# The last product of a two-block layer by Strassen's scheme, with a wider 31-tap convolution and the third mixer moved ahead

## The chip, the cores and the metric

One core of one Trainium2 chip runs the kernel. The metric is the device time of one launch in microseconds (us). A median of three launches is given for the kernel before.

## The reference

Two blocks follow one another on x (1024 tokens by 1024 channels, fp32). The first is a hybrid attention layer with an MLP. The second, which the change touches, reads

```python
proj = h @ w_in_2                                  # 1024 x 1024 times 1024 x 5632, eleven slots of 512
(va, za, bb, bc, bv, zb, ca, cg, zc, dv, zd) = split(proj, 11)
ya = rglru(va);  yb = bb * conv3(bc * bv)
yc = silu(layer_norm(conv31(ca * sigmoid(cg)))) @ c_pw + c_pw_b
yd = (grouped product of pool_grid(dv)) * d_scale
cat = concat([ya * silu(za), yb * silu(zb), yc * silu(zc), yd * silu(zd)])   # 1024 x 2048
x = x + gate * (cat @ w_out_2)                     # 1024 x 2048 times 2048 x 1024: the last product
return rms_norm(x, final_g)
```

The four mixers are called a, b, c and d; c, the third, holds the 31-tap convolution, the layer norm and the product with `c_pw`.

## The kernel before, in words

Channels lie on the 128 partitions and tokens on the free axis, in two halves of 512. Every fp32 product is taken as three float32r matmuls: an operand is split into a high part (a copy on ACT that rounds) and a low part (a subtraction on DVE), and high times high, high times low and low times high go into one PSUM bank (`mm3_steps`, lines 411 to 413). So each 128x128 block of weights costs three matmuls per half of the tokens, and each 128x1024 tile of weights costs one split (`split`, L367 on ACT and L368 on DVE) after a 512 KB load on SP's queue (`load_raw`, L372). `take` keeps one tile of weights prepared ahead in the order of `weight_order`; three raw and three split tiles exist.

`mixers_in` makes the eleven slots: 44 column blocks, each a projection `p2` of 8 x 3 matmuls per half. The work of the mixers is laid between them by hand: generators stand in two lists, and after each projection `fill(FA, FB)` lets the first list, `self.bg` (mixers a and d, chunk by chunk), run for FA units and the second, `convs` (four 31-tap convolutions), for FB. A generator yields the units that a step stands for. `conv31` (L1986 to L1997) holds its two accumulators of 128x512 in PSUM (`pp`, five banks), makes two instructions of DVE a tap (L1994), 30 taps after the first, and copies the result back over its input on ACT. Mixer c starts when the loop over mixer b reaches its last chunk: what is left of the convolutions is run out, then `mixer_c` goes on `self.bg`, and what is not done by the end goes on in the last product. The framework orders the instructions of each engine by this program order and by when they are ready; instructions marked `pin` keep their place.

All mixers store 128x512 tiles of `cat` in DRAM (`cat_out`, `cat_store`; a factor 0.5 belongs to the silu). `tail` is the last product: `dense(pair, hf, ticks)` loads eight `cat` tiles (L2196, `cr`), splits them (`cx`, L467 and L468), and for each of eight column blocks n makes one projection of 24 matmuls and adds it, times the gate (`MOD`), to x (L2208). Two pairs of mixers, (a, d) and (b, c), and two halves of the tokens give four calls, 32 projections, 768 matmuls. x comes back from DRAM by `load_x` (`x2d`); the second pair also sums squares (`add_sq`, L1362 and L1363); `final` normalises (L2218) and stores. The product of the MLP earlier in the kernel already goes by Strassen's scheme, with sums of weight blocks made by `weight_sums`: a DMA on GpSimd's queue (POOL) loads a block into the one tile `ws`, others add to it in flight, and others store the sums to DRAM (L1490, L1494, L1496). `pace` emits one of these DMAs per projected half. 32 tiles of 128x1024 (`S`) and small pools of eight (`T2`) and six (`F2`) 128x512 tiles hold everything.

Of the kernel before, what the change touches and what calls it, by code (L numbers as in the profile page):

```python
# [17 lines left out]
P = 128  # L18
# [10 lines left out]
NL, N1, N2, N4, N3, FA, FB = 6.0, 3.0, 3.0, 2.4, 2.5, 4.0, 3.0  # L29
# [272 lines left out]
class Build:  # L302
    def __init__(self, tc, ctx, A, out, dbg=None):
# [16 lines left out]
        self.sums, self.paced = self.weight_sums(), 0  # L320
# [54 lines left out]
    def load_w(self, src, w=T):  # L375
# [3 lines left out]
        self.split(raw[:, :w], hi[:, :w], lo[:, :w])  # L379
        return hi, lo  # L380

    def weight_order(self):
# [9 lines left out]
        q += [("wo2", pair, n) for pair in range(2) for hf in range(2) for n in range(8)]  # L392
        self.wq, self.ahead = q, []

    def take(self, *key):
        if self.wq[0] is None:
            self.wq.pop(0)
        assert self.wq.pop(0) == key
        load = lambda name, *i: self.load_w(self.A[name][i] if name == "wup" else
                                               self.A[name][i].rearrange("p k n -> p (k n)"))  # L400
# [1079 lines left out]
    def weight_sums(self):  # L1480

        nc = self.nc
        A = self.A["wm2"]
        self.ws = {n: [self.dp.tile([P, T], F32, name=f"{n}w{j}") for j in range(8)] for n in ("S1", "S2", "S3", "S4")}
        pin = self.tc.keep_in_program_order
        for j in range(8):
            block = lambda a, b: A[a, b][:, j * T:j * T + T]
            for first, *terms in (((1, 0), (1, 1), "S1", (0, 0), "S2", (0, 1), "S4"), ((0, 0), (1, 0), "S3")):
                t = self.wsp.tile([P, T], F32, tag="ws", name=self.nm("ws"))
                pin(nc.gpsimd.dma_start(t, block(*first)))  # L1490
                yield
                for x in terms:
                    if isinstance(x, str):
                        pin(nc.gpsimd.dma_start(self.ws[x][j], t))  # L1494
                    else:
                        pin(nc.gpsimd.dma_start(t, block(*x), accum_op=ALU.add))  # L1496
                    yield
# [470 lines left out]
    def cat_out(self, i, c, y, z, hf):  # L1968
# [3 lines left out]
        self.nc.vector.scalar_tensor_tensor(t, y, 0.5, t, op0=ALU.mult, op1=ALU.mult)  # L1972
        self.cat_store(i, c, t, hf)

# [5 lines left out]
    def conv31(self, c, u):  # L1980

        nc = self.nc
        w = lambda j: self.CW[:, 31 * c + j:31 * c + j + 1]
# [250 lines left out]
def run(gen):  # L2234
    for _ in gen:
        pass
# [48 lines left out]
```

## Time and profile before

| | us |
|---|---|
| median of 3 launches (lowest, highest) | 2552.47 (2544.95, 2559.07) |
| the profiled launch | 2546.38 |
| its span, first to last instruction | 2544.6 |
| PE busy | 2462.2 (97%) |
| DVE busy | 1726.1 (68%) |
| ACT busy | 1193.8 (47%) |
| POOL busy | 181.9 (7%) |

PE is TensorE, PEld its weight loads, DVE is VectorE, ACT is ScalarE, POOL is GpSimd, SP is the engine that issues most DMAs. A matmul's row is longer than the time until the next one starts, since they are pipelined, so a pace is read from starts and not from durations. The mean granted clock of TensorE is 0.984 of full speed, 1.00 in all windows from 1813 us until the last matmul.

### The profile page before, as it was taken

To read this page: it belongs to the slowest core of one execution; us is meant where nothing else is said; L and a number is where in the kernel's file an instruction comes from. 1 tells how busy PE (TensorE), PEld (TensorE's weight loads), DVE (VectorE), ACT (ScalarE), POOL (GpSimd) and SP (SyncE) were. 2 spreads that over 40 slices of the span, in tenths; PEclk is the share of its full clock that TensorE was granted. 3 is DMA by queue.
4 is the path that set the end of the run, shared out by engine and by line. 5 is a ranking of instruction groups with operands and counts; after the bars stand their busy time and mean duration, and the time that the engine had idled before them with its cause. 6 is when DMAs were issued, how large, how long until landed. Compare 5 with 4: busy or idle time off the path is not lost. (4 is left out here: it accounts for less than half of the span.)

```text
span 2544.6 us, 33697 instructions
## 1 busy us (share of the span) xinstructions
PE 2462.2 (97%) x12692; PEld 1996.6 (78%) x12692; DVE 1726.1 (68%) x2647; ACT 1193.8 (47%) x1848; POOL 181.9 (7%) x238
## 2 busy tenths in 40 slices
PE   8989999999989999999999999999999999999997
PEld 6878898777777678877788888887888888887786
DVE  7537566574755436758867864468798999996744
ACT  6425554622514358146744543435536355445623
POOL 0000000120211111630000000000000000000000
PEclk9989999999999999999999999999999999999999
DMA  6364453584774567859676565556533333325732
GB/s 223 105 212 138 129 152 114 163 242 118 218 220 145 184 208 235 301 174 281 229 263 223 173 212 169 195 184 229 186 117 113 133 134 98 112 92 195 243 100 100
DMA packets 180084, 449.23 MB, mean 177 GB/s; under 512 B 32144, under 2 KB 42256, under 8 KB 179920
## 3 DMA queue, kind: packets, MB, share of 16 engines
q1 hardware_dynamic: 141504, 342.44, 40.7%
q0 software_dynamic: 18576, 64.63, 9.2%
q10 hardware_dynamic: 19840, 40.00, 4.2%
q8 instruction: 100, 1.64, 0.3%
q14 instruction: 64, 0.52, 0.1%
HBM read 321.55 MB, written 125.44 MB: 176 GB/s over the span
## 5 line engine op out<-in xcount | busy, mean ns | idle before, releaser
L367 ACT CAST wh<-wr 128x1024 fp32r<-128x1024 f32 (+1 forms) x243 | 254.8, 1049 | 481.6 <-PE mm L412 231.1
L368 DVE TENSOR_TENSOR wl<-wr,wh 128x1024 fp32r<-128x1024 f32 (+1 forms) x243 | 298.6, 1229 | 180.9 <-ACT wh L367 172.4
L411 PE MATMUL mm<-h,wh 128*128 128x512 f32 x736 | 301.2, 410 | 7.1 <-ACT h L467 4.3
L412 PE MATMUL mm<-h,wh 128*128 128x512 f32 x736 | 298.0, 405 | 0.0
L413 PE MATMUL mm<-h,wl 128*128 128x512 f32 x736 | 295.9, 402 | 0.3 <-DVE wl L368 0.3
L411 PE MATMUL mm<-kk,wh 128*128 128x512 f32 x704 | 275.2, 391 | 0.0
L412 PE MATMUL mm<-kk,wh 128*128 128x512 f32 x704 | 274.5, 390 | 0.5 <-DVE kk L1784 0.5
L413 PE MATMUL mm<-kk,wl 128*128 128x512 f32 x704 | 274.0, 389 | 0.0
L411 PEld LDWEIGHTS mm<-h,wh 128*128 128x128 f32 x736 | 141.8, 193 | 39.7 <-ACT h L467 5.9
L412 PEld LDWEIGHTS mm<-h,wh 128*128 128x128 f32 x736 | 141.8, 193 | 32.4 <-issue 3.6
L1994 DVE SCALAR_TENSOR_TENSOR pp<-cu,vec,pp 128x512 f32<-128x512 f32 (+9 forms) x240 | 166.7, 749 | 0.1
L413 PEld LDWEIGHTS mm<-h,wl 128*128 128x128 f32 x736 | 141.1, 192 | 32.6 <-issue 1.8
L412 PEld LDWEIGHTS mm<-kk,wh 128*128 128x128 f32 x704 | 132.1, 188 | 29.2 <-issue 1.0
L411 PEld LDWEIGHTS mm<-kk,wh 128*128 128x128 f32 x704 | 132.1, 188 | 28.3 <-issue 0.7
L413 PEld LDWEIGHTS mm<-kk,wl 128*128 128x128 f32 x704 | 132.1, 188 | 27.6 <-issue 0.2
L1512 PE MATMUL pp<-h,wh 128*128 128x512 f32 x320 | 127.1, 400 | 3.0 <-ACT x L1579 2.2
L1513 PE MATMUL pp<-h,wh 128*128 128x512 f32 x320 | 125.0, 391 | 1.4 <-DVE h L468 1.4
L1514 PE MATMUL pp<-h,wl 128*128 128x512 f32 x320 | 123.9, 390 | 0.0
L1721 PE MATMUL pp<-bl,wh 128*128 128x512 f32 x304 | 119.3, 392 | 2.3 <-DVE bl L468 1.6
L1722 PE MATMUL pp<-bh,wl 128*128 128x512 f32 x304 | 118.4, 389 | 0.0
L1720 PE MATMUL pp<-bh,wh 128*128 128x512 f32 x304 | 116.4, 391 | 1.6 <-ACT bh L472 1.6
L411 PE MATMUL mm<-cx,wh 128*128 128x512 f32 x256 | 99.8, 391 | 1.3 <-ACT cx L467 1.3
(559 smaller groups left out, 5453.2 us busy)
## 6 DMA issues: line engine op xcount, KB each, us to landing
wr<-in_wi_dram SPq DMA_DIRECT2D x77, 512.0 KB, 3.7
ws<-in_wm_dram POOLq DMA_DIRECT2D x48, 512.0 KB, 5.9
wr<-in_wo_dram SPq DMA_DIRECT2D x48, 512.0 KB, 3.7
wr<-in_wg_dram SPq DMA_DIRECT2D x32, 512.0 KB, 4.6
gt<-gt POOLq DMA_DIRECT2D x64, 256.0 KB, 3.6
g<-gt SPq DMA_DIRECT2D x64, 256.0 KB, 5.2
wm<-in_wm_dram SPq DMA_DIRECT2D x32, 512.0 KB, 5.0
br<-buB SPq DMA_DIRECT2D x32, 512.0 KB, 4.5
```

Of the source, the lines that this page charges most:

```text
L367: self.nc.scalar.copy(hi, raw)
L368: self.nc.vector.tensor_sub(lo, raw, hi.bitcast(F32))
L411: M(ps, lhsT=ah, rhs=bh, start=start and i == 0, stop=False)
L412: M(ps, lhsT=ah, rhs=bl, start=False, stop=False)
L413: M(ps, lhsT=al, rhs=bh, start=False, stop=stop and i == last)
L1512: M(ps, lhsT=ah, rhs=bh, start=start and i == 0, stop=False, skip_group_check=True)
L1513: M(ps, lhsT=ah, rhs=bl, start=False, stop=False, skip_group_check=True)
L1514: M(ps, lhsT=al, rhs=bh, start=False, stop=i == last, skip_group_check=True)
L1720: M(banks[p], lhsT=wh[:, o], rhs=bh[:, r], start=first, stop=False, skip_group_check=True)
L1721: M(banks[p], lhsT=wh[:, o], rhs=bl[:, r], start=False, stop=False, skip_group_check=True)
L1722: M(banks[p], lhsT=wl[:, o], rhs=bh[:, r], start=False, stop=jj == 7 and e == 1, skip_group_check=True)
L1994: nc.vector.scalar_tensor_tensor(o, u[:, a + s:b + s], w(j), o, op0=ALU.mult, op1=ALU.add)
```

## The change

Four edits.

1. **The last product.** `cat` and `w_out` are cut into 2 x 2 blocks: rows by pair of mixers, columns of tokens by half, columns of the output by half. Seven products P1, P5, P2, P6, P7, P4, P3 of 4 column blocks x 8 x 3 matmuls take the place of eight. The sums of weight blocks (S1 to S4) are made by `weight_sums`, now with its count and block as arguments, in DRAM during `mixers_in`. The sums of `cat` blocks are made by DMAs: SP loads a tile, and a DMA on POOL's queue adds the other block to it. Four of the sixteen block quarters are stored with the other sign (`half_of`). Products are added to x straight from PSUM, each wherever it belongs (`add`): P1 to three places, P5 to two, the others to one. P2 is accumulated in the banks of P1, and P7 and P4 in those of P6.
2. **The convolution.** One accumulator of 128x1024 in SBUF (`co`), one instruction of up to 1024 columns a tap; the first tap is ACT's; the copy back goes.
3. **The third mixer.** `mixer_c` stands in `convs` behind the four convolutions; what is left at the end goes to `self.bg`.
4. **The rates.** FA 4.0 to 4.2, FB 3.0 to 4.4.

```diff
-NL, N1, N2, N4, N3, FA, FB = 6.0, 3.0, 3.0, 2.4, 2.5, 4.0, 3.0
+NL, N1, N2, N4, N3, FA, FB = 6.0, 3.0, 3.0, 2.4, 2.5, 4.2, 4.4
...
+        src = {"P1": lambda: block(0, j), "P2": lambda: block(1, j), "P4": lambda: block(1, 4 + j),
+               "P5": lambda: self.ws["S1"][j], "P6": lambda: self.ws["S2"][j], "P7": lambda: self.ws["S3"][j],
+               "P3": lambda: self.ws["S4"][j]}[p]()
+        return self.load_w(src, minus=p == "P2")
...
-        q += [("wo2", pair, n) for pair in range(2) for hf in range(2) for n in range(8)]
+        q += [("o2", p, j) for p in ("P1", "P5", "P2", "P6", "P7", "P4", "P3") for j in range(4)]
...
-    def conv31(self, c, u):
+    def conv31(self, c, us):
...
-        acc = [self.pp(), self.pp()]
-        for hf, sl in enumerate(HS):
-            nc.vector.tensor_scalar(acc[hf], u[:, sl], w(15), None, op0=ALU.mult)
+        o = self.S("co")
+        nc.scalar.mul(o, u, w(15))
...
-            for hf in range(2):
-                a, b = max(HALF * hf, -s), min(HALF * hf + HALF, T - s)
-                o = acc[hf][:, a - HALF * hf:b - HALF * hf]
-                nc.vector.scalar_tensor_tensor(o, u[:, a + s:b + s], w(j), o, op0=ALU.mult, op1=ALU.add)
-            yield 1.3
-        for hf, sl in enumerate(HS):
-            nc.scalar.copy(u[:, sl], acc[hf])
+            a, b = max(0, -s), min(T, T - s)
+            nc.vector.scalar_tensor_tensor(o[:, a:b], u[:, a + s:b + s], w(j), o[:, a:b], op0=ALU.mult, op1=ALU.add)
+            yield 1.2
+        us[c] = o
...
+        self.sums = self.weight_sums(4, lambda a, b, j: self.A["wo2"][b, 4 * a + j].rearrange("p k n -> p (k n)"))
...
+            convs.append(self.conv31(c, cus))
+            if c == 3:
+                convs.append(self.mixer_c(cus))
...
-            if c == 3:
-                while convs:
-                    self.tick(1, convs)
-                self.behind(self.mixer_c(cus))
...
+        self.bg += convs
...
+        def source(p, k):
+            if p in ("P1", "P2", "P3", "P7"):
+                t = self.F2("cr")
+                nc.sync.dma_start(t, cat(*{"P1": (0, 0), "P2": (1, 0), "P3": (1, 1), "P7": (0, 1)}[p], k))
+                if p == "P7":
+                    nc.gpsimd.dma_start(t, cat(1, 1, k), accum_op=ALU.add)
+                return t
+            t = part(k)
+            if p == "P5" and k not in made:
+                nc.sync.dma_start(t, cat(0, 1, k))
+            elif p == "P5":
+                return t
+            made.add(k)
+            nc.gpsimd.dma_start(t, cat(*{"P5": (0, 0), "P6": (1, 1), "P4": (1, 0)}[p], k), accum_op=ALU.add)
+            return t
...
+        for k in range(8):
+            source("P5", k)
+        run(ops["P1"])
+        run(ops["P5"])
+        A = bank_a()
+        for hf in (1, 0):
+            self.load_x(x, hf, lambda hf, j: self.x2d[hf][j])
+        for j, ps in product("P1", bs["P1"], A, True, (), 5):
+            add(1, 0, j, ps)
+            add(1, 1, j, ps)
+            add(0, 1, j, ps, True)
+        for j, ps in product("P5", bs["P5"], None, True, (), 5):
+            add(1, 1, j, ps)
+            add(0, 1, j, ps, True)
         self.flush()
-        dense(1, 0, 0)
+        run(ops["P2"])
+        for j, ps in product("P2", bs["P2"], A, False, ops["P6"]):
+            add(0, 0, j, ps, True, True)
+        A = bank_a()
+        for j, ps in product("P6", bs["P6"], A, True, ops["P7"]):
+            add(0, 1, j, ps)
+        for j, ps in product("P7", bs["P7"], A, False, ops["P4"]):
+            add(1, 1, j, ps, True, True)
+        for j, ps in product("P4", bs["P4"], A, False, ops["P3"]):
+            add(1, 0, j, ps, True, True)
         self.behind(final(0))
-        dense(1, 1, 2)
+        for j, ps in product("P3", bs["P3"], None, True, (), 3):
+            add(0, 1, j, ps, True, True)
         self.flush()
         run(final(1))
```

## Rows read from the trace of the kernel before

**Rows 1.** Page, part 1: busy time, share of the span, instructions of each engine.

```profile
PE 2462.2 (97%) x12692; PEld 1996.6 (78%) x12692; DVE 1726.1 (68%) x2647; ACT 1193.8 (47%) x1848; POOL 181.9 (7%) x238
```

**Rows 2.** Windows: stretch, length, busy us and instructions by engine, clock, DMA share, GB/s.

```profile
1813.00:2334.00 521.00, 517.32 (x2263) 423.38 (x2263) 474.64 (x611) 249.49 (x330) 14.84 (x20) 1.00 0.36 121
1956.00:2276.00 320.00, 318.32 (x1399) 261.66 (x1398) 305.38 (x383) 148.84 (x197) 13.68 (x18) 1.00 0.34 116
2276.00:2334.00 58.00, 56.66 (x246) 45.65 (x245) 43.55 (x62) 28.24 (x42) 0.00 (x0) 1.00 0.35 120
2334.00:2424.00 90.00, 88.56 (x384) 71.66 (x385) 64.18 (x91) 51.09 (x76) 0.00 (x0) 1.00 0.73 255
2424.00:2529.00 105.00, 105.00 (x464) 86.56 (x462) 48.14 (x57) 30.50 (x36) 0.00 (x0) 1.00 0.28 93
```

**Rows 3.** Tile `cx`: count, duration ns min/median/max, first and last start, forms.

```profile
L411 PE MATMUL mm<-cx,wh x256: 389/389/798, 2333.9 to 2528.5; 128*128 128x512 f32 x128
L413 PE MATMUL mm<-cx,wl x256: 387/389/796, 2334.9 to 2529.0; 128*128 128x512 f32 x128
```

**Rows 4.** Timeline of PE, 30 matmuls apart: start us, duration us.

```profile
2503.16 0.39 PE L413 MATMUL mm<-cx,wl 128*128 128x512 f32 x1
...
2509.96 0.39 PE L413 MATMUL mm<-cx,wl 128*128 128x512 f32 x1
```

**Rows 5.** Chain of work that ended last, from the last epilogue.

```profile
2529.42 0.76 DVE x L2208
...
2536.92 3.98 DVE x L2218 x6
```

**Rows 6.** Groups by form, 1700 us on: busy us, mean ns, idle before.

```profile
L368 DVE TENSOR_TENSOR wl<-wr,wh 128x1024 fp32r<-128x1024 f32 x101 | 123.6, 1223 | 28.8 <-ACT wh L367 24.2 <-DMA wr<-S1w 2.9
L468 DVE TENSOR_TENSOR cx<-cr,cx 128x512 fp32r<-128x512 f32 x32 | 20.2, 687 | 5.3 <-ACT cx L467 5.3
L2208 DVE SCALAR_TENSOR_TENSOR x<-mm,MOD,x 128x512 f32<-128x512 f32 x32 | 24.0, 750 | 59.3 <-PE mm L413 59.3
```

**Rows 7.** The same view: the convolution's instructions, and a sum without PSUM.

```profile
L1994 DVE SCALAR_TENSOR_TENSOR pp<-cu,vec,pp 128x512 f32<-128x512 f32 x120 | 89.7, 753 | 0.0
L1986 DVE TENSOR_SCALAR pp<-cu,vec 128x512 f32<-128x512 f32 x8 | 5.7, 749 | 0.0
L2218 DVE SCALAR_TENSOR_TENSOR x<-x,vec,rs 128x512 f32<-128x512 f32 x16 | 11.0, 748 | 7.2 <-ACT rs L448 7.2
```

**Rows 8.** Timeline of DVE: six narrow taps in a row, and what follows.

```profile
2285.49 4.00 DVE L1994 SCALAR_TENSOR_TENSOR pp<-cu,vec,pp 128x512 f32<-128x512 f32 x6
2289.39 1.23 DVE L368 TENSOR_TENSOR wl<-wr,wh 128x1024 fp32r<-128x1024 f32 x1
```

**Rows 9.** Timeline of DVE: wide taps, first with another between, then dependent neighbours.

```profile
2205.26 1.28 DVE L1823 SCALAR_TENSOR_TENSOR xc<-va,vec,xc 128x1023 f32<-128x1023 f32 x1
2206.45 0.74 DVE L1994 SCALAR_TENSOR_TENSOR pp<-cu,vec,pp 128x502 f32<-128x502 f32 x1
...
2306.31 1.28 DVE L2052 SCALAR_TENSOR_TENSOR by<-bm,vec,by 128x1023 f32<-128x1023 f32 x1
2307.63 1.28 DVE L2053 SCALAR_TENSOR_TENSOR by<-bm,vec,by 128x1023 f32<-128x1023 f32 x1
```

**Rows 10.** Windows inside the last product, columns as in rows 2.

```profile
2340.00:2350.00 10.00, 10.00 (x46) 8.29 (x45) 5.86 (x8) 3.46 (x5) 0.00 (x0) 1.00 1.01 375
...
2390.00:2400.00 10.00, 10.00 (x46) 8.29 (x45) 5.44 (x8) 3.83 (x6) 0.00 (x0) 1.00 1.00 355
```

**Rows 11.** Lines 1496 (adding DMA) and 1490 (plain): issue ns, then landing us.

```profile
L1496 POOL DMA_DIRECT2D ws<-in_wm_dram x32: 878/922/957, 470.8 to 1188.2; - x32
...
DMA to landing us min/median/max: 5.5/6.6/9.7
...
L1490 POOL DMA_DIRECT2D ws<-in_wm_dram x16: 527/538/541, 465.3 to 1183.7; - x16
...
DMA to landing us min/median/max: 4.1/4.7/7.9
```

More of the change, by code (lines that the diff above doesn't have):

```diff
@@ L319, in __init__ @@
         self.wsp = e(tc.tile_pool(name="wsp", bufs=1))
-        self.sums, self.paced = self.weight_sums(), 0
+        self.sums, self.paced = self.weight_sums(8, lambda a, b, j: A["wm2"][a, b][:, j * T:j * T + T]), 0
     def dma(self, dst, src, q="sync"):
@@ L378, in load_w @@
         lo = self.wp.tile([P, T], F32R, tag="wl", name=self.nm("wl"))
-        self.split(raw[:, :w], hi[:, :w], lo[:, :w])
+        (self.hilo_minus if minus else self.split)(raw[:, :w], hi[:, :w], lo[:, :w])
         return hi, lo
@@ L2188, in tail @@
         accs = [None, None]
[L2190 to L2211 removed]
+        run(self.sums)
@@ new lines, in tail, with part @@
+        ng = self.sm(8)
+        nc.vector.tensor_scalar(ng, self.MOD[:, 16:24, 0], -1.0, None, op0=ALU.mult)
+        cat = lambda b, c, k: self.cat[((0, 3), (1, 2))[b][k // 4], k % 4, c]
+        ct, made = [], set()
+        def part(k):
+            if k % 2 == 0 and len(ct) <= k // 2:
+                ct.append(self.S("ct"))
+            return ct[k // 2][:, HS[k % 2]]
+        def source(p, k):
[13 more added lines that the diff above has]
+            return t
@@ new lines, in operand, with add @@
+        def operand(p, bs):
+            for k in range(8):
+                t = self.S("cx", F32R)
+                (self.hilo_minus if p in ("P7", "P4") else self.hilo)(source(p, k), t[:, 0:HALF], t[:, HALF:T])
+                bs.append(t)
+                if k % 2:
+                    yield
+        def add(a, c, j, ps, minus=False, done=False):
+            n = 4 * a + j
+            xa = x.get(n, c)
+            nc.vector.scalar_tensor_tensor(xa, ps, ng[:, n:n + 1] if minus else self.MOD[:, 16 + n, 0:1], xa,
+                                           op0=ALU.mult, op1=ALU.add)
+            if done:
+                first = accs[c] is None
+                if first:
+                    accs[c] = self.T2("acc")
+                self.add_sq(accs[c], xa, first)
@@ new lines, in product @@
+        def product(p, bs, banks, start, ahead=(), ticks=0):
+            M = nc.tensor.matmul
+            for j in range(4):
+                w = self.cols(self.take("o2", p, j))
+                ps = banks[j] if banks else self.mm()
+                for k in range(8):
+                    h, l = bs[k][:, 0:HALF], bs[k][:, HALF:T]
+                    M(ps, lhsT=w[0][k], rhs=h, start=start and k == 0, stop=False, skip_group_check=True)
+                    M(ps, lhsT=w[0][k], rhs=l, start=False, stop=False, skip_group_check=True)
+                    M(ps, lhsT=w[1][k], rhs=h, start=False, stop=k == 7, skip_group_check=True)
+                yield j, ps
+                next(iter(ahead), None)
```

62 lines of the change are left out of this document (24 added, 38 removed).

## The prediction

> **What bounds the kernel now.** The page's busy times come first [rows 1]: PE is busy 97% of the span, DVE 68%, POOL 7%. So time is to be had only from fewer matmuls or from the 3% in which PE waits. The windows then show the two stages that the change touches [rows 2]. In the mixers' stage (1813 to 2334 us) PE is busy 517.3 of 521.0 us, and in its middle DVE is nearly as full: 305.4 of 320. In the last product PE idles 1.4 of the first 90 us and nothing of the next 105, with DVE at 64.2 and 48.1. So PE bounds both stages, with DVE close behind in the first and far behind in the second. The granted clock is 1.00 in all of them, so the change can win or lose nothing there as long as PE stays busy. The chain that ended last closes with a piece that the change leaves alone: from the last epilogue at 2529.4 us to the end at 2544.6 us, 15.2 us of sums of squares, normalisation and stores [rows 5].
>
> **The matmuls.** Before, the last product has 32 projections of 24 matmuls, 768 (three lines of 256 each, first start 2333.9 us, last 2529.0) [rows 3]. After, it has 7 products x 4 x 24 = 672, so 96 go. The price of one is its pace: 30 matmuls take 2509.96 - 2503.16 = 6.80 us, 0.2267 us each [rows 4]. That is **-21.8 us**, all on the path, because PE bounds this stage. The third mixer's own matmuls move from this stage to the one before and cost the same there.
>
> **Waits that may go.** PE idles 3.7 us in the mixers' stage and 1.4 us in the last product [rows 2]. At most 5.1 us can come back. I take -2: the third mixer's chain no longer runs through the last product, and P1 needs only mixers a and d, finished earlier. **-2 us.**
>
> **Vector work of the last product, beside PE.** Sums into x go from 32 to 40 (12 for P1, 8 for P5, 4 for each other product), +8 x 0.75 = 6.0 us; operand splits from 32 to 56, +24 x 0.69 = 16.5; weight splits from 32 to 28, -4 x 1.22 = -4.9 [rows 6]. The third mixer takes away what else lies in the first 90 us: 64.2 less 16 weight splits (19.6), 32 operand splits (22.0) and 16 sums (12.0) leaves 10.6 [rows 2, 6]. So DVE has 64.2 + 48.1 + 17.6 - 10.6 = 119 us of work in 672 x 0.2267 = 152 us, and in P1 with P5, the fullest, 16 splits, 8 weight tiles and 20 sums make 35.8 of 43.5 us. ACT has less: 82 of 195 us before [rows 2], and one side of each new split. This costs nothing while PE has 18 to 22% of room above it; without the room it would be the excess of DVE over PE.
>
> **Boundaries between products.** Each product needs eight new operands, and the low parts queue on DVE behind the last sum of the product before. P6 to P3 have theirs spread under the product before; P2 has all eight after P5's sums. The lower bound is nothing, since before the last product loses 1.4 us at three such boundaries [rows 2]. The upper is one sum and one split at each of six, 6 x (0.75 + 0.69) = 8.6 us [rows 6]. Nearest is the row of before, with twice the boundaries: **+3 us.**
>
> **DMAs of the last product.** Its start asks for much at once. For P1, P5 and P2 I count 6.5 MB of weights, 4 of x, 2 + 2 added for P5, 2 for P1, 2 for P2, 2 added for P6, 3 for P7: 23.5 MB. Windows at a full DMA share show 355 to 375 GB/s [rows 10]. An adding DMA lands in 6.6 us where a plain one takes 4.7 [rows 11], so 5.5 MB count 1.4 times: 25.7 MB, 72 us at 355 GB/s, against 65 us of PE. But the 6 MB of P1 and P5 need only mixers a and d, so they can be issued under the last projections, where the DMA share is 0.35 [rows 2]: 54 us then. Hence 0 to 7 us; full windows before also leave PE busy [rows 10], so I take **+2 us.** On SP's queue the eight loads of P5 stand before P1's; on POOL's, 8 adding issues of 0.92 us each for P5, P6, P7 and P4, 29 us in 152, with nothing else there [rows 11].
>
> [...]
>
> **The wide convolution.** Before, a tap is two instructions of 0.75 us [rows 7], but neighbours overlap: six take 2289.39 - 2285.49 = 3.90 us, 0.65 each [rows 8], 1.30 a tap. After, a tap is one instruction of 1.28 us. With another instruction between, the next starts 1.19 us later; where the neighbour needs its result, 1.32 us [rows 9]. Successive taps need each other's result, so the price is 1.19 to 1.32, and 120 taps win 13 us of DVE or lose 2. Eight first taps (5.2 us) go to ACT as four wide ones in place of eight copies back. I take 1.26, about -10 us of DVE with the first taps, in a stage where PE bounds: nothing on the path by itself.
>
> [...]
>
> **The third mixer ahead, and the rates.** A fill issued three tap steps of two instructions, 6 x 0.65 = 3.9 us of DVE; now it issues four of 1.19 to 1.32, 4.8 to 5.3. That is 0.9 to 1.4 us more for each of the 25 fills that the convolutions then last (100 steps after the first 20), 22 to 35 us in a stretch where DVE idled 14.6 of 320 us [rows 2]; the third mixer follows in the next fills. The excess of 8 to 20 us delays background first. It reaches PE when the low part of a weight is late, and that is prepared one projection ahead, 48 x 0.2267 = 10.9 us. So 0 to 10 us; after it come four projections almost without background, which win nothing back for PE. The row of before at 95% shows PE losing 1.7 in 320 us, and I take **+4 us.**
>
> **Weight sums.** Forty DMAs on POOL's queue, one per projected half, behind which mixer d's clears and a load wait. A sum waits for the landing before it, 4.7 to 6.6 us [rows 11]; POOL was busy 14.8 of 521 us [rows 2]. Mixer d is background: 0 to 3 us, taken as **+0.5 us.** The 20 MB fit in a DMA share of 0.36.
>
> **Sum.** -21.8 - 2 + 3 + 2 + 4 + 0.5 = -14.3 us. The profiled launch took 2546.4 us, so 2532.1; the median of before is 6.1 us above that launch, so on its footing **2538 us**, 0.6% less.
>
> **Rivals.**
> - *The DMAs bound the first three products* (17%). For it: share 1.00 in windows of before, x and all operands at once. Against: PE did not wait in those windows. Price: 7 us by the rows if nothing is issued early, 17 if an adding DMA counts twice, in place of my 2: 2538 + 5 to 15, 2543 to 2553, no change at the middle.
> - *The third mixer leaves holes in a full DVE* (14%), the slower end. Its chain goes back and forth between ACT, DVE and PE. From 2276 to 2334 us, where it ran, DVE idled 14.5 of 58 us [rows 2]. Two halves of the tokens make 29 us of holes, now where the convolutions and mixer a leave no slack; taps at 1.32 add some 8. Against: other work can fill holes, and no engine order of the new kernel is known. If none is filled: -14.3 - 4 + 37 = +19, 2571 us. It decides once DVE idles over 18 us there while PE waits for a weight's low part.
> - *The third mixer is not ahead after all* (8%): tiles run short (32 of 128x1024, one more per convolution), so it slips into the last product, and P2 waits for its `cat`. Half of it, 48 matmuls and their chain, some 11 to 15 us of PE idle: 2549 to 2553.
> - *Nothing is lost anywhere* (6%): -21.8 - 5.1 = -26.9, 2526 us.
>
> **How the numbers follow.** My forecast gets 55%. A measurement of this kernel can tell about 0.5%, 13 us, from no change. The forecast's own bounds are -26.9 below and -21.8 + 8.6 + 7 + 10 + 3 = +7 above, 2526 to 2560. Low ends at 2518, since launches before spread 7 us below their median; the high end at 2562 cuts the slower rival only. Faster by over 0.5% gets 0.47 of my forecast's 0.55, all of the best case and 0.04 of the DMA rival; slower 0.02 of mine, 0.13 of the second rival; the rest is no change.
>
> **What would show it.** In the changed profile: 672 matmuls of `cx` at a pace of 0.2267 us in about 157 us; 15 us after the last; DVE over 95% in the mixers' middle with PE losing about 6 us; convolution taps of 1.28 us; no third mixer in the last product; a DMA share under 1.00 in most of P1 to P2. I am wrong if PE idles over 20 us more than before in these stages, or if the last product with its end still takes more than 195 us.

## The result and the profile after

| | before | after |
|---|---|---|
| median of the launches timed side by side, us | 2547.77 | 2566.39 |
| lowest to highest, us | 2542.77 to 2559.07 | 2561.63 to 2575.52 |
| the profiled launch, us | 2546.38 | 2575.52 |
| its span, us | 2544.6 | 2573.7 |

The ratio is **1.0077, with a 95% interval of 1.0057 to 1.0097**: 0.8% slower, where the prediction said 0.6% faster, and outside its range. The profiled launch of the changed kernel is the slowest of its nine, 9.1 us above their median, so the parts read from it below add up to more than the medians differ by (29.1 us of span against 18.6). First the page of the changed kernel, part 1, which answers to [rows 1], then the windows for [rows 2], with the middle of the mixers' stage (1860 to 2260) as a window of its own.

```profile
PE 2463.4 (96%) x12596; PEld 1989.4 (77%) x12596; DVE 1723.4 (67%) x2548; ACT 1199.9 (47%) x1863; POOL 238.0 (9%) x310
```

```profile
1818.00:2386.00 568.00, 547.11 (x2341) 442.13 (x2339) 477.89 (x517) 269.10 (x357) 30.14 (x40) 0.98 0.42 137
1860.00:2260.00 400.00, 385.73 (x1661) 313.05 (x1660) 364.98 (x368) 180.12 (x236) 19.34 (x27) 0.99 0.38 124
2340.00:2386.00 46.00, 40.66 (x165) 32.54 (x164) 22.34 (x31) 15.15 (x22) 7.08 (x8) 0.93 0.76 224
2386.00:2424.00 38.00, 33.63 (x145) 27.09 (x146) 20.61 (x31) 16.06 (x28) 7.18 (x8) 0.99 1.00 308
2424.00:2559.00 135.00, 127.52 (x530) 102.59 (x529) 84.62 (x114) 52.95 (x74) 14.18 (x16) 0.94 0.54 153
```

The same middle window of the kernel before:

```profile
1860.00:2260.00 400.00, 398.79 (x1751) 327.41 (x1749) 376.34 (x475) 188.49 (x247) 14.31 (x19) 1.00 0.34 116
```

The 96 matmuls are gone (12596 against 12692), but PE's busy time has not fallen. In the middle of the mixers' stage DVE has 11 us less to do than before, and PE makes 90 matmuls less in the same 400 us. The clock is no longer 1.00 in any of these stretches.

Tile `cx`, the last product, for [rows 3]: 160 and 64 of each line, 672 in all, from 2386.2 to 2558.5 us.

```profile
L2257 PE MATMUL pp<-cx,wh x160: 388/389/795, 2386.2 to 2535.4; 128*128 128x512 f32 x160
L2259 PE MATMUL mm<-cx,wl x64: 388/389/628, 2408.9 to 2558.5; 128*128 128x512 f32 x64
```

The pace, for [rows 4], 30 matmuls apart, where nothing disturbs PE (2506.61 - 2499.81 = 6.80 us, 0.2267 each, as before):

```profile
2499.81 0.39 PE L2259 MATMUL pp<-cx,wl 128*128 128x512 f32 x1
...
2506.61 0.39 PE L2259 MATMUL pp<-cx,wl 128*128 128x512 f32 x1
```

The end of the chain, for [rows 5]: from the last sum at 2558.92 us to the end of the span 14.8 us, against 15.2 before.

```profile
2558.92 0.76 DVE x L2242
```

Groups of DVE from 1700 us on (all lengths of a tap in one line), for [rows 6, 7]: sums and splits cost what they cost, and a wide tap 1.27 us.

```profile
L2006 DVE SCALAR_TENSOR_TENSOR co<-cu,vec,co 128x1009 f32<-128x1009 f32 (+14 forms) x120 | 152.5, 1270 | 4.8 <-ACT co L2000 4.0
L368 DVE TENSOR_TENSOR wl<-wr,wh 128x1024 fp32r<-128x1024 f32 x94 | 114.5, 1220 | 34.1 <-ACT wh L367 30.9 <-ACT rr L1842 2.1
L478 DVE TENSOR_TENSOR cx<-cr,cx 128x512 fp32r<-128x512 f32 x24 | 15.5, 686 | 1.6 <-ACT cx L477 1.5
L2242 DVE SCALAR_TENSOR_TENSOR x<-pp,sm,x 128x512 f32<-128x512 f32 x16 | 12.0, 747 | 21.0 <-PE pp L2259 20.9
```

**Where the time went.** Take two stretches: the *stage*, from the first matmul on `kk` (1812.4 us before, 1818.0 after) to the first on `cx` (2333.9, 2386.2), and the *product*, from there to the last on `cx` (2529.0, 2558.5). The stage went from 521.5 to 568.2 us, the product from 195.1 to 172.3. The third mixer's matmuls that lay in the product before are 384 + 464 - 768 = 80 [rows 2], 18.1 us at the pace. So the stage should have taken 539.6 and lost 28.6; the product should have taken 672 x 0.2267 = 152.3 and lost 20.0. (The stage starts 5.6 us later. Ahead of it the change has only 28 of the forty DMAs of its weight sums, which ran from 1208 to 1397 us. The fifteen profiled launches with these DMAs start the stage at 1808.2 to 1822.6, 1814.8 on the mean, the five without at 1809.1 to 1817.6, 1813.0 on the mean: no cost that can be told from the spread.)

Three places hold these losses. In the middle of the stage PE waits mostly for DVE (waits of PE in 1860 to 2260: total us, times, longest):

```profile
PE mm L423 <- DVE wl L368: 8.4, 5, 2.2
PE pp L421 <- ACT xh L477: 2.9, 2, 2.6
PE pp L422 <- DVE pl L478: 1.8, 2, 1.5
```

At the handover, from 2340 to 2386 us, PE makes 165 matmuls where 203 fit (8.6 us), and in the product it idles 4.4 us by 2424 and 7.5 after. Windows of 10 us over both, then PE's waits in 2360 to 2430:

```profile
2350.00:2360.00 10.00, 10.00 (x45) 8.14 (x45) 6.07 (x10) 3.00 (x4) 5.33 (x6) 1.00 0.97 297
2360.00:2370.00 10.00, 7.74 (x34) 6.06 (x33) 0.83 (x1) 0.69 (x1) 1.74 (x2) 1.00 1.11 261
2370.00:2380.00 10.00, 7.17 (x19) 5.65 (x20) 3.17 (x5) 1.80 (x3) 0.00 (x0) 0.66 0.85 280
...
2410.00:2420.00 10.00, 9.50 (x42) 7.52 (x41) 1.08 (x2) 0.00 (x0) 0.00 (x0) 1.00 1.07 324
2420.00:2430.00 10.00, 2.85 (x5) 1.44 (x6) 10.00 (x16) 6.33 (x9) 0.00 (x0) 0.67 0.41 163
```

```profile
PE pp L421 <- ACT wch L367: 5.1, 1, 5.1
PE mm L2257 <- ACT wh L367: 4.2, 1, 4.2
PE mm L2257 <- DVE x L2242: 3.5, 1, 3.5
```

The DMA share is at its top (0.97 to 1.11) for some 10 us, then PE stops: it waits for the last weights of the third mixer (`wcr`, `wch`), and later for S1's weights and for x, which the first sums need. What ACT and DVE wait for from 2330 to 2430 us shows that these are late out of the DMA queues:

```profile
ACT wh L367 <- DMA wr<-S1w: 15.6, 2, 15.4
DVE x L2242 <- DMA x<-x2d: 12.4, 1, 12.4
ACT wch L367 <- DMA wcr<-in_wcp_dram: 10.6, 2, 9.1
```

The third loss is the clock. One wait in the mixers' stage, on PE's timeline: after 2.60 us without work, matmuls start 0.43 us apart in place of 0.2267.

```profile
2034.86 0.39 PE L422 MATMUL mm<-kk,wh 128*128 128x512 f32 x1
2037.85 1.22 PE L421 MATMUL pp<-xh,abh 128*128 128x512 f32 x2 [2.60 <-ACT xh L477]
...
2039.30 0.63 PE L421 MATMUL mm<-kk,wh 128*128 128x512 f32 x1
2039.72 0.63 PE L422 MATMUL mm<-kk,wh 128*128 128x512 f32 x1
```

That is 0.2267 / 0.43 = 0.53 of the pace; the granted clock from 2037.8 to 2041.0 us is 0.50. In the middle window 13.1 us more idle time than before come with 90 x 0.2267 = 20.4 us of missing matmuls. Three of its four stretches of 100 us, with the granted clock behind the engines:

```profile
1860.00:1960.00 100.00, 99.03 (x434) 80.77 (x433) 81.95 (x79) 45.62 (x58) 1.16 (x2) 1.00 0.33 109
1960.00:2060.00 100.00, 95.86 (x413) 77.96 (x413) 89.52 (x92) 39.90 (x57) 11.92 (x17) 0.98 0.64 190
2160.00:2260.00 100.00, 95.35 (x401) 76.47 (x400) 96.20 (x101) 49.94 (x64) 3.71 (x5) 0.97 0.25 90
```

A granted clock of 0.98 and 0.97 in two of the four, and 1.00 in the others, can take at most 2 + 3 = 5 us of the 7.3 between the two. The rest is not the clock's: a wait shows shorter than it is, since the matmul ahead of it counts as busy for 0.39 us where the next would have started after 0.2267 (above, 2037.85 - 2034.86 = 2.99 us from start to start, 2.76 over the pace, for 2.60 of idle time). In the product 11.9 us of idle time come with 20.0 lost, and there the granted clock of 0.99 and 0.94 in its two windows can take at most 0.4 + 8.1 = 8.5 us.

### The profile page after: what moved, and what is told of

It is laid out like the page before. It is cut to its first block, busy times and chain, and to the rows that moved or that the text cites. A ratio compares the mean times of both kernels' runs of the same rounds, so it can differ in the third digit from the quotient of the medians.

```text
span 2573.7 us, 33553 instructions
## 1 busy us (share of the span) xinstructions
PE 2463.4 (96%) x12596; PEld 1989.4 (77%) x12596; DVE 1723.4 (67%) x2548; ACT 1199.9 (47%) x1863; POOL 238.0 (9%) x310
## 5 line engine op out<-in xcount | busy, mean ns | idle before, releaser
L367 ACT CAST wh<-wr 128x1024 fp32r<-128x1024 f32 (+1 forms) x235 | 246.1, 1049 | 425.4 <-PE mm L422 132.3
L368 DVE TENSOR_TENSOR wl<-wr,wh 128x1024 fp32r<-128x1024 f32 (+1 forms) x235 | 288.3, 1228 | 183.8 <-ACT wh L367 177.0
L422 PEld LDWEIGHTS mm<-h,wh 128*128 128x128 f32 x736 | 143.0, 194 | 32.6 <-issue 3.6
L423 PEld LDWEIGHTS mm<-kk,wl 128*128 128x128 f32 x704 | 133.3, 189 | 39.0 <-DVE wl L368 10.6
L2006 DVE SCALAR_TENSOR_TENSOR co<-cu,vec,co 128x1009 f32<-128x1009 f32 (+14 forms) x120 | 152.5, 1270 | 4.8 <-ACT co L2000 4.0
L1279 ACT ACTIVATE gt<-mm,bgh 128x512 f32<-128x512 f32 x64 | 43.5, 683 | 99.3 <-PE mm L423 98.9
```

Source lines behind the costliest of these rows:

```text
L367: self.nc.scalar.copy(hi, raw)
L368: self.nc.vector.tensor_sub(lo, raw, hi.bitcast(F32))
L422: M(ps, lhsT=ah, rhs=bl, start=False, stop=False)
L423: M(ps, lhsT=al, rhs=bh, start=False, stop=stop and i == last)
L2006: nc.vector.scalar_tensor_tensor(o[:, a:b], u[:, a + s:b + s], w(j), o[:, a:b], op0=ALU.mult, op1=ALU.add)
```

## The experiments

The theory: two causes that have nothing to do with each other. The adding DMAs load the DMA engines twice as much as plain ones (1.92 times per MB, below), which starves the handover and P1 to P2; and DVE, given four taps a fill, delivers low parts of weights late. The rivals: the third mixer's place is the cause and not the rate; the order of the DMAs is the cause and not their kind. All runs in one table (times in us; "middle" is the count of PE's instructions between 1860 and 2260):

| run | stage | middle | product | median | ratio to before, 95% |
|---|---|---|---|---|---|
| before | 521.5 | 1751 | 195.1 | | |
| the change | 568.2 | 1661 | 172.3 | 2566.39 | 1.0077 (1.0057 to 1.0097) |
| e2_mixers_only | 556.0 | 1679 | 175.4 | 2562.73 | 1.0045 (1.0029 to 1.0061) |
| e3_product_only | 548.3 | 1750 | 189.6 | 2569.61 | 1.0066 (1.0045 to 1.0088) |
| e5_wide_taps_only | 525.3 | 1745 | 195.1 | 2553.74 | 1.0025 (1.0010 to 1.0040) |
| e10_wide_and_ahead | 521.8 | 1745 | 208.0 | 2562.67 | 1.0065 (1.0045 to 1.0085) |
| e11_wide_and_rates | 542.1 | 1672 | 192.8 | 2565.88 | 1.0066 (1.0045 to 1.0086) |
| e1_lower_rate | 565.0 | 1665 | 171.4 | 2565.78 | 1.0066 (1.0047 to 1.0084) |
| e4_narrow_taps | 577.2 | 1654 | 172.4 | 2581.75 | 1.0110 (1.0074 to 1.0146) |
| e7_no_adding_dmas | 558.2 | 1672 | 153.8 | 2541.09 | 0.9979 (0.9961 to 0.9998) |
| e8_hold_back_adds | 563.8 | 1668 | 167.5 | 2562.05 | 1.0070 (1.0052 to 1.0089) |
| e9_sums_on_gpsimd | 559.7 | 1668 | 166.3 | 2559.30 | 1.0045 (1.0021 to 1.0070) |
| e15_sums_on_vector | 554.8 | 1682 | 156.1 | 2546.55 | 1.0004 (0.9985 to 1.0023) |
| e12_sums_on_gpsimd_late | 538.8 | 1745 | 192.8 | 2565.16 | 1.0069 (1.0047 to 1.0091) |
| e14_p5_under_p1 | 560.9 | 1656 | 193.9 | 2583.97 | 1.0141 (1.0109 to 1.0174) |
| e16_alternating_rate | 571.5 | 1735 | 168.2 | 2570.02 | 1.0092 (1.0074 to 1.0109) |
| e18_vector_and_alternating | 559.1 | 1735 | 163.4 | 2552.92 | 1.0029 (1.0013 to 1.0045) |
| e19_three_taps_bare_mixer | 604.9 | 1717 | 153.8 | 2588.00 | 1.0163 (1.0143 to 1.0183) |
| e20_taps_early | 568.4 | 1672 | 157.4 | 2558.64 | 1.0041 (1.0024 to 1.0059) |
| e21_taps_early_less | 570.6 | 1684 | 153.7 | 2557.22 | 1.0033 (1.0015 to 1.0050) |

**The halves of the change.** `e2_mixers_only` is the kernel before with edits 2 to 4, `e3_product_only` the kernel before with edit 1.

```diff
 e2, against the changed kernel
-        q += [("o2", p, j) for p in ("P1", "P5", "P2", "P6", "P7", "P4", "P3") for j in range(4)]
+        q += [("wo2", pair, n) for pair in range(2) for hf in range(2) for n in range(8)]
... (and the rest of edit 1 taken back)
 e3, against the changed kernel
-NL, N1, N2, N4, N3, FA, FB = 6.0, 3.0, 3.0, 2.4, 2.5, 4.2, 4.4
+NL, N1, N2, N4, N3, FA, FB = 6.0, 3.0, 3.0, 2.4, 2.5, 4.0, 3.0
...
+                self.behind(self.mixer_c(cus))
... (and the rest of edits 2 and 3 taken back)
```

> The kernel before with edits 2, 3 and 4 alone (wide taps, third mixer behind the convolutions, rates 4.2 and 4.4); the last product as before, without weight sums. Theory A (most of the loss is DVE, filled by the higher rate and the third mixer while PE waits for low parts of weights): PE idles some 10 us or more between 1960 and 2260 us as in the changed kernel (13 us idle there), the last product gains a little because the third mixer is gone, and the whole is 10 to 20 us slower than before. Theory B (the loss is the DMAs of the last product and of the weight sums): the mixers' stage loses under 5 us against before and the whole is the same as before within 5 us.

> The kernel before with edit 1 alone (Strassen's scheme, weight sums in DRAM, adding DMAs); convolution, third mixer and rates as before. Theory A (DVE in the mixers' stage): the middle of the mixers' stage runs as before, and with 96 matmuls fewer the whole is 5 to 20 us faster than before, less what the last product loses. Theory B (DMAs): the last product still idles 15 to 25 us, with x and the weight sums landing 10 us late, so that the whole is within 6 us of before or slower, since part of the third mixer also comes back into it.

Each half alone is slower than before. Seven runs have the changed kernel's mixers' stage as it is (the change, `e1`, `e7`, `e8`, `e9`, `e14`, `e15`), and their middle counts lie between 1656 and 1682: differences of up to 26 matmuls, 5.9 us, tell nothing. With the mixers' edits alone the middle has 1679, so the loss there has nothing to do with Strassen's scheme or its DMAs. With the product alone the middle is as before (1750), so the weight sums cost it nothing, with twelve of their forty DMAs in it; but stage and product together take 548.3 + 189.6 = 737.9 us, where the kernel before, less the 96 matmuls, would take 716.6 - 21.8 = 694.8. Both halves hold a loss of their own.

**Taps: width, place and rate.**

```diff
 e5, against the kernel before: the new conv31, and
-            convs.append(self.conv31(c, cus[c]))
+            convs.append(self.conv31(c, cus))
 e10, against e2
-NL, N1, N2, N4, N3, FA, FB = 6.0, 3.0, 3.0, 2.4, 2.5, 4.2, 4.4
+NL, N1, N2, N4, N3, FA, FB = 6.0, 3.0, 3.0, 2.4, 2.5, 4.0, 3.0
 e11, against e5
-NL, N1, N2, N4, N3, FA, FB = 6.0, 3.0, 3.0, 2.4, 2.5, 4.0, 3.0
+NL, N1, N2, N4, N3, FA, FB = 6.0, 3.0, 3.0, 2.4, 2.5, 4.2, 4.4
```

> The kernel before with edit 2 alone: wide taps into a 128x1024 tile, the rates and the third mixer's place as before, the last product as before. With edits 2 to 4 together PE lost about 20 us between 1860 and 2260 us. If the wide taps alone do it (their accumulator takes one of the 32 large tiles, and a tap is twice as long in front of a weight's low part), PE's count of matmuls from 1860 to 2260 us falls from 1751 to 1690 or less and the whole is 5 to 12 us slower than before. If the third mixer's place or the rates do it, the stage runs as before (1740 or more) and the whole is the same within 4 us.

> The kernel before with the wide convolution and the third mixer ahead, but three taps a fill as in the kernel before, and the last product as before. If the third mixer's place costs the 20 us between 1860 and 2260, TensorE has some 1680 matmuls there (as with edits 2 to 4 together: 1679), the stage from first to last kk lasts some 550 us, and the time is some 2562. If the rate of taps (four a fill) costs it, some 1740 matmuls lie there (wide taps alone: 1745), the stage is some 535 (18 us of it the third mixer's own matmuls), and the time is some 2550 or under.

> The kernel before with the wide convolution and the new rates (four taps a fill), the third mixer left at its old place, and the last product as before. If the rate costs the 20 us, some 1680 to 1700 matmuls lie between 1860 and 2260 and the time is some 2560 or more, less what taps that end earlier give back at the third mixer. If the third mixer's place costs it, some 1745 matmuls and the time of the wide taps alone, 2553.

The middle counts separate cleanly: 1751, 1745 and 1745 at three taps a fill, 1672, 1679 and 1661 at four, wherever the third mixer stands, and the gap is far over the 26 by which runs of one stage differ. So **the rate costs the middle, not the place**. PE's waits there, with three taps (`e5`) and with four (`e11`), the rates being all that differs:

```profile
PE pp L411 <- ACT ph L467: 1.1, 1, 1.1
PE pp L412 <- DVE pl L468: 0.9, 1, 0.9
```

```profile
PE mm L413 <- DVE wl L368: 7.9, 4, 2.2
PE pp L412 <- DVE pl L468: 1.8, 2, 1.5
```

`e10` was meant to test the place by itself, and can't: at three taps a fill nothing of the third mixer gets done ahead. In its trace the third mixer's products run inside the last product, later than before (2319.1 to 2405.5 in the kernel before), and the product takes 13 us longer:

```profile
L411 PE MATMUL pp<-sc,wch x32: 387/389/628, 2340.9 to 2426.2; 128*128 128x512 f32 x32
```

So edit 3 needs edit 4. The wide taps alone cost 6 us where nothing was expected, although they take 10.6 us off DVE in the middle (376.3 to 365.8); their profiled launch shows 3.8 us of it in the stage, and what makes it so is open.

**Lower rate, narrow taps.** Two edits of the changed kernel.

```diff
 e1
-NL, N1, N2, N4, N3, FA, FB = 6.0, 3.0, 3.0, 2.4, 2.5, 4.2, 4.4
+NL, N1, N2, N4, N3, FA, FB = 6.0, 3.0, 3.0, 2.4, 2.5, 4.2, 3.6
 e4: conv31 as before, two instructions a tap
-            yield 1.2
+            yield 1.3
```

> The changed kernel with FB 3.6 instead of 4.4: three wide taps a fill (3.6 us of DVE) instead of four (4.8 us), so the convolutions last 33 fills and the third mixer falls into the last fills and the last product. Theory A (DVE overfilled by the rate): PE's idle time from 1960 to 2260 us falls from 13 us to under 5 and the whole is 5 to 12 us faster than the changed kernel. Theory B (DMAs of the last product): the last product is as slow or slower, and the whole gains under 3 us.

> The changed kernel with the convolution of before (two accumulators of 128x512 in PSUM, two instructions a tap, 1.3 units, 4 taps a fill). If the wide taps cost DVE time, this is faster than the changed kernel by up to 10 us; if the wide taps are worth what their starts say (1.19 us a tap against 1.30), it is slower by 5 to 15 us, since DVE is full where they run and gets 120 x 0.11 = 13 us and the first taps' 5 us more.

`e1` tells nothing: three taps of 1.2 units leave a remainder in floating point that is just over nothing, so a fill of 3.6 still issues a fourth tap, and the run repeats the changed kernel (1665 in the middle, the same time). `e4` is slower than the change, by 8 us by the ratios (1.0110 against 1.0077) and 15 by the medians; the intervals overlap, so the size is open. Its trace goes the same way: at four taps a fill DVE has 379.6 us of work in the middle in place of 365.0, and PE's waits for `wl` in the stage are 13.6 us in place of 8.4. So the wide taps seem worth having at the higher rate only.

**The adding DMAs.** `e7` leaves the 32 adding DMAs out, and so the sums of `cat` blocks: P5, P6, P7 and P4 get one block each. `e8` holds P6's back until P5's first sums: POOL issues them 32.6 us after the first matmul on `cx`, in place of 8.2. `e9` and `e15` put a plain load and an addition on GpSimd or VectorE in their place.

```diff
 e7, in source()
-                if p == "P7":
-                    nc.gpsimd.dma_start(t, cat(1, 1, k), accum_op=ALU.add)
...
-            nc.gpsimd.dma_start(t, cat(*{"P5": (0, 0), "P6": (1, 1), "P4": (1, 0)}[p], k), accum_op=ALU.add)
 e8, ahead of P2; the adding DMAs keep program order behind it
+            pin(nc.gpsimd.tensor_copy(self.sm(1), x.get(n, c)[:, 0:1]))
...
+        gate(0, 1)
 e9, in place of each adding DMA (e15: nc.vector)
+            r = self.T2("ca")
+            nc.sync.dma_start(r, d)
+            nc.gpsimd.tensor_add(t, t, r)
```

> The changed kernel without the 32 adding DMAs of the last product: the sums of cat blocks are left out, all else stays (24 of the 56 operands are then one block instead of two). If the DMAs are what the last product waits for (adding ones cost twice a plain one's time on the engines), it takes under 160 us from its first to its last matmul instead of 172, x lands in time, and the whole is 12 to 25 us faster than the changed kernel. If the boundaries between products (operands late on DVE and ACT) are the cause, it stays above 167 us and the whole gains under 6 us.

> The changed kernel, with one tiny copy on POOL that waits for the last sum of P5 ahead of the adding DMAs of P6, so that these (and those of P7 and P4 behind them) can't go out during P1 as they do in the changed kernel, where x and the weight sums of P5 landed 15 us late. If it is the early adds that hold x and the weights back, x lands in time, PE's wait of some 9 us after 2419 us goes, and the whole is 5 to 12 us faster; against it, P6 and P7 get their adds later, and if the adds are slow the wait only moves there (no change).

> The changed kernel with the sums of cat blocks made by GpSimd: both blocks come by plain loads on SP's queue, and one addition of 128x512 on POOL takes the place of each adding DMA. If adding DMAs cost twice a plain one's time, the last product's DMA share falls and it takes under 165 us instead of 172, the whole 5 to 15 us faster than the changed kernel; if the number of loads in SP's queue or buffers of 128x512 bind, it is the same or slower.

> The changed kernel with the sums of cat's blocks added by VectorE from plain loads, in place of the adding DMAs. With them added by GpSimd the time was 2559, without any 2541. If those 18 us are GpSimd's (ops of VectorE that run beside GpSimd's additions last longer: 8 of them fill 10 us in 2460:2470), VectorE's own additions, 32 of some 0.7 us, cost little: the product lasts under 160 us and the time is 2541 to 2550. If they are the second loads (32 of 256 KB), the product stays at 165 or more and the time at 2555 or more.

Without them the kernel is 25 us faster (1.0077 - 0.9979 = 0.0098 of 2547), in the profiled launches 18.5 in the product and 10 in the stage. Most of the 10 are at the handover, where PE makes 198 matmuls in the 46 us up to the first `cx` in place of 165 (7.5 us), with the granted clock at 1.00:

```profile
2330.00:2376.00 46.00, 45.24 (x198) 36.53 (x197) 26.70 (x37) 22.36 (x33) 0.00 (x0) 1.00 0.55 192
```

Its product takes 153.8 us against 152.3 of bare matmuls: in the product Strassen's saving is whole once these DMAs are gone. What one costs stands in the DMA queues of the changed kernel from 2340 to 2480 us (q1 holds the plain ones, q0 the adding ones; packets, MB, share of 16 engines):

```profile
q1 hardware_dynamic: 9936, 23.86, 48.9%
q0 software_dynamic: 4608, 8.39, 33.0%
```

48.9 / 23.86 = 2.05% of that time for a plain MB, 33.0 / 8.39 = 3.93% for an added one: **1.92 times**. A rival is that POOL's queue makes a DMA dear and not the adding. The weight sums settle it, since their plain DMAs use the same queue q0. Here are a plain load (1982.3 to 1987.0 us of the changed kernel) and an adding one of the same size (1987.0 to 1994.7), each alone on q0:

```profile
q0 software_dynamic: 144, 0.52, 41.2%
q0 software_dynamic: 144, 0.52, 43.2%
```

The plain one took 41.2% of 4.7 us, 1.9 us of all 16 engines, and the adding one 43.2% of 7.7 us, 3.3. The other four from 1972 to 2004 us are alike: two plain stores 1.3 each, two adding loads 3.0 and 3.3. At SP's price, 2.05% of 140 us a MB, 0.52 MB would be 1.5. Holding P6's back gives 2 to 4 us (1.0070 against 1.0077, 2562.05 against 2566.39), which the runs can't tell from nothing. Then the same traffic in plain loads: with the additions on VectorE the same stretch shows

```profile
q1 hardware_dynamic: 14679, 34.28, 69.2%
```

in place of 48.9 + 33.0 = 81.9%, and the kernel is back at the time of before (1.0004), with the product at 156.1: the second loads and 32 sums on VectorE cost 2.3 us there. So the cost was the adding in the DMA, and not the bytes. GpSimd is a worse place for it (1.0045), and its rows show splits of VectorE that last longer (groups of `e9` from 2370 to 2550 us):

```profile
L2216 POOL TENSOR_TENSOR ct<-ct,ca 128x512 f32<-128x512 f32 x24 | 37.9, 1599 | 157.0 <-DMA ca<-cat 155.1 <-DVE cx L478 1.9
L478 DVE TENSOR_TENSOR cx<-ct,cx 128x512 fp32r<-128x512 f32 x16 | 14.6, 953 | 2.2 <-ACT cx L477 1.8
L483 DVE SCALAR_TENSOR_TENSOR cx<-cr,cx 128x512 fp32r<-128x512 f32 x8 | 10.0, 1282 | 0.0
L2247 DVE SCALAR_TENSOR_TENSOR x<-pp,sm,x 128x512 f32<-128x512 f32 x16 | 11.9, 745 | 9.2 <-PE pp L2264 9.2
```

Beside GpSimd's additions these splits of VectorE take 953 and 1282 ns on the mean; in `e15`, without GpSimd, the same two groups take 687 and 686. The sums from PSUM stay at 745. What couples the two engines is not shown.

**P5 under P1.**

```diff
 e14, against the changed kernel (e12: the same in e3, with GpSimd's sums of e9)
-        for k in range(8):
-            source("P5", k)
...
-        run(ops["P5"])
...
-        for j, ps in product("P1", bs["P1"], A, True, (), 5):
+        for j, ps in product("P1", bs["P1"], A, True, ops["P5"], 5):
```

> The mixers' stage of the kernel before with the Strassen product of the changed one, its operand sums added by GpSimd from plain loads, and P5's operands fetched under P1 in place of under the third mixer. If the 31 us between the last kk and the first cx of the product alone came from P5's transfers beside the third mixer's last weights, that gap falls to 5 to 8 us, the product stays at 155 to 170, and the time is 2515 to 2535: under both kernels. If the third mixer and the product have another wait in common (the ScalarE copies of the weights), the gap stays at 20 or more and the time at 2555 or more.

> The changed kernel, adding DMAs and all, with P5's operands fetched under P1 in place of under the third mixer. If the handover's loss comes from those transfers, TensorE waits less than 2 us for the third mixer's last weights in 2340 to 2386 (10 in the changed kernel), and the time falls by 8 to 12 us to some 2555. But P6's adding DMAs then stand behind P5's in the queue: by the rival that the adding DMAs as a whole are the cost, the wait shows in P1 and P5 instead, and the time stays within 4 us of 2566.

Both miss. `e14` is 16 us slower than the change: the wait for the third mixer's weights is gone from the handover (stage 7 us shorter), but the adding DMAs now come due inside P1, and PE waits for the operands. Its waits in 2370 to 2575:

```profile
PE mm L2257 <- ACT cx L477: 16.3, 4, 5.8
```

So in `e14` the place of these loads moves the wait, as the rival said. `e12` has a stage 9.5 us shorter than `e3` and a product 3.2 longer (its additions are GpSimd's, too), but from the last `kk` to the first `cx` it still takes 21.7 us (31.0 in `e3`), within the bounds that its expectation gave to another wait that the third mixer and the product have in common. Which one, and so most of `e3`'s loss, is open.

**Keeping PE fed in the mixers' stage.** Five attempts at a rate that loses neither the middle nor the third mixer.

```diff
 e16 (the change) and e18 (e15), in fill(): three and four taps by turns
-            self.tick(b, convs)
+            self.tick(3.0 if fills[0] > 4 and fills[0] % 2 else b, convs)
... (`fills[0]` counts the calls)
 e19 (e15): three, and the rest of the third mixer ahead of the product
-NL, N1, N2, N4, N3, FA, FB = 6.0, 3.0, 3.0, 2.4, 2.5, 4.2, 4.4
+NL, N1, N2, N4, N3, FA, FB = 6.0, 3.0, 3.0, 2.4, 2.5, 4.2, 3.0
...
-        self.bg += convs
+        while convs:
+            self.tick(1, convs)
 e20 (e15), in fill(): the same taps, more of them early
+        rates = [8.3] * 4 + [5.9] * 8 + [3.5, 4.4] * 14
...
-            self.tick(b, convs)
+            self.tick(rates.pop(0), convs)
 e21
+        rates = [6] * 4 + [5.9] * 12 + [3.5, 4.4] * 12
```

> The changed kernel, adding DMAs and all, with three and four taps a fill by turns, in place of four always; what is left of the third mixer goes behind what follows. If four taps a fill cost the 20 us of the mixers' stage, 1700 or more matmuls lie between 1860 and 2260 (1661 in the changed kernel) and the time is 2556 to 2562. If VectorE's work is too late in any order, the matmuls stay under 1680 and the time within 4 us of 2566.

> The two edits before this together: sums on VectorE and three and four taps a fill by turns. By the theory that the rate and the adding DMAs are the two costs, and that they lie at different places, the gains add up: 2532 to 2543, under the kernel before. By the rival (each gain is eaten by the other's stage) it stays at 2548 or over.

> Sums on VectorE, three taps a fill throughout as in the kernel before, and what is left of the third mixer issued by itself ahead of the product. The middle of the stage must then lose nothing: 1740 or more matmuls between 1860 and 2260. What is left of the third mixer costs by itself 25 to 35 us from the last kk to the first cx (31 us with the product alone), and the time is 2540 to 2555. If fewer than 1700 matmuls lie in the middle, the rate isn't the cause.

> Sums on VectorE as in e15, and as many taps as there (four a fill on the mean), but more of them early, where VectorE idles (some 33 of 40 us busy between 1900 and 1980), and fewer late, where it is full: seven in each of the first four fills, five in eight, then three and four by turns. If the 16 us lost between 1860 and 2260 are VectorE's work bunched late, 1715 or more matmuls lie there (1682 in e15), the third mixer is still ahead, and the time is 2535 to 2542: under both kernels. If VectorE has no real slack early (what is idle there is ahead of work that must come first), the matmuls stay at 1660 to 1690 and the time within 4 us of 2546.

> As the run before, with the first four fills as in the changed kernel, five taps in the twelve after them, then three and four by turns. By the theory of idle VectorE early, something between e15 and the run before: 2538 to 2546. By the rival no change, or a loss in 1860 to 1980 where five taps (6 us) and the rest of VectorE's work outlast a projection of 48 matmuls (10.9 us).

The rate decides the middle again: 1735 at three and four by turns, 1717 at three (with one 4 us wait that `e5` doesn't have; 18 matmuls), all over the 1682 that four reaches at most; and since FA stays at 4.2 in these runs, it is FB that counts. But what isn't done then is paid at the handover, bare and at a lower granted clock (in `e18` 0.79 from 2340 to 2380 us; in `e19` 0.71 from 2340 to 2380 and 0.65 from 2380 to 2420): from the last `kk` to the first `cx` it is 3.5 us in the change, 42 in `e16`, 30 in `e18`, 82 in `e19`. The gains don't add up: `e18` is no faster than `e15`, as the rival said. Taps laid early fill DVE early (40.0 of 40 us from 1940 on in `e20`) and PE stops there instead:

```profile
1940.00:1980.00 40.00, 40.00 (x178) 32.95 (x177) 40.00 (x39) 22.53 (x28) 5.37 (x7) 1.00 0.48 160
1980.00:2020.00 40.00, 31.91 (x120) 25.28 (x119) 40.00 (x41) 10.64 (x15) 5.39 (x8) 0.87 0.71 197
```

`e21` keeps the middle count of four taps (1684) and takes 25 us from the last `kk` to the first `cx`. In no order tried does the third mixer fit in this stage for nothing. No version with the whole product beats the kernel before; `e15` draws level with it. The kernel before with edit 1 alone and its sums on VectorE was not run.

## Why the prediction was wrong

The stage and the product together were to change by -14.3 us and changed by 740.5 - 716.6 = +23.9 in the profiled launches, a miss of 38.2. `e7` parts it, in the profiled launches again: the adding DMAs cost 740.5 - 712.0 = 28.5 where the sum had +2, and what remains without them, 712.0 - (716.6 - 21.8) = 17.2, stood in the sum as -2 + 3 + 4 + 0.5 = 5.5. The misses are 26.5 and 11.7.

- **The matmuls, -21.8: right.** 672 remain, the pace is the same, and `e7` has its product in 153.8 us.
- **DMAs of the last product, +2: the step that failed most.** "So 5.5 MB count 1.4 times" read the price from two landing times [rows 11]. Landing times went from 4.7 to 6.6 us, 1.4 times; the time of the DMA engines per MB went up 1.92 times. The price alone is not the miss: at 1.92 the step's sum is 28.6 MB and 80 us, 15 over PE's 65. The second half of the step failed too: P5's DMAs can be issued under the last projections, and were, but just there the third mixer's last weights were due (7.5 us at the handover), and the granted clock was 0.66 and 0.67 in the windows of PE's waits (2370 to 2380, 2420 to 2430 us). The rival of the DMAs named the mechanism, at 17% and at 5 to 15 us. Its 17 us are the same sum with 5.5 MB counted twice (29 MB, 82 us at 355 GB/s, less 65); no row of before shows that factor, and the trace of after shows 1.92.
- **The third mixer ahead and the rates, +4: mechanism right, size wrong.** "It reaches PE when the low part of a weight is late" is what `e11` and the change show; the bound of 10 us was too low. In the change the middle loses 20.4 us, in `e15` the stage loses 554.8 - 539.6 = 15.2. The step spread an excess of DVE work over the stage and let the lead of one projection absorb it; DVE in the middle did less than before (365.0 of 400 us) and still was late: it was busy for 82 of the middle's first 100 us and 96 of its last, where PE made 434 and 401 matmuls. The rival of holes had its sign to show (DVE idle 35 us there while PE waits for `wl`) and gave 2571. But it laid the holes to the third mixer's chain, and `e11` has the loss with that mixer at its old place; that its 2571 lies near the 2566 measured is luck.
- **The clock: a term left out.** "The change can win or lose nothing there as long as PE stays busy" held its own condition; in the change PE waits up to 2.6 us at a time in the middle and up to 4.2 in the product, and a granted clock of 0.97 and 0.94 in stretches there took up to 5 us in the middle and up to 8.5 in the product (20.0 lost, 11.9 idle). How long a wait lowers it is not shown: `e15` waits up to 2.2 us at a time in the middle, with the clock at 1.00.
- **Boundaries and vector work: right.** The product lost 1.5 us in `e7`, 3.8 in `e15` with 32 more instructions on DVE. **Weight sums, +0.5:** `e3`'s middle shows no cost, but 28 of the forty DMAs ran hundreds of us ahead of the stage that the step put them in, so it was hardly put to the test. **Waits that may go, -2:** no run tells them from the rest.
- **The wide convolution: the price right, its effect not.** Seven taps in a row start (1920.06 - 1911.00) / 7 = 1.29 us apart, in the bounds of 1.19 to 1.32, and `e5` shows DVE 10.6 us lighter; but alone it costs 6 us (3 to 10), not 0.

```profile
1911.00 9.14 DVE L2006 SCALAR_TENSOR_TENSOR co<-cu,vec,co 128x1018 f32<-128x1018 f32 x7
1920.06 1.22 DVE L368 TENSOR_TENSOR wl<-wr,wh 128x1024 fp32r<-128x1024 f32 x1
```

## What to carry to other kernels

Price a DMA that adds by its queue's share per byte in a full stretch, not by its landing time, and where an engine has room give it the sum: 32 additions of 0.69 us on VectorE brought back some 19 us here (1.0077 to 1.0004). Where PE is nearly full, a helper's mean busy share says little; ask how much of its work is issued between two results that PE needs. Such waits cost more than the idle time they show: 20.4 us of matmuls for 13.1 more of idle time in the change, whose granted clock is 0.99 there, and still 15.6 (69 matmuls) for 11.6 in `e15`, whose granted clock is 1.00 all through the middle. An edit that moves work ahead of a boundary needs a place that is empty in the right windows: here each rate either starved PE in the stage or left the work bare at its end.

## What the runs showed of the hardware

- An adding DMA took 1.92 times the DMA time of a plain one per MB (3.93% against 2.05% of the same 140 us). On POOL's queue alone, a plain load of 0.52 MB took 1.9 us of all 16 engines and an adding one 3.3.
- After a wait of 2.60 us matmuls started 0.43 us apart in place of 0.2267 until 2041.0 us; the granted clock was 0.50 from 2037.8 to 2041.0 us, and 0.89 on the mean of the 10 us from 2030.
- VectorE's 128x512 splits with both inputs in SBUF took 831 to 1282 ns on the mean in place of 686 to 688 (`e15`) in a stretch where GpSimd added tiles in SBUF (`e9`, 1599 ns each); sums with one input in PSUM stayed at 745 ns.
